# Merge projection of a hybrid decoder layer: from a direct product to Strassen's seven products, with the feed-forward start reordered

## The chip, the cores and the metric

One core of a Trainium2 chip runs the whole kernel. Time is device microseconds of that core for one launch. The engines are TensorE (PE, with its weight loads PEld), VectorE (DVE), ScalarE (ACT), GpSimd (POOL) and SyncE (SP, which here only issues DMAs).

## The reference

The kernel computes one layer for a prompt of 1024 tokens and 8 sample tokens that share the weights, and returns states and caches besides. The part that matters here:

```python
merged = g_a * y_a + g_b * y_b + g_c * y_c          # three gated branches
x = x + merged @ w_merge_o                          # 1024 x 1024
xn = rmsnorm(x, norm_ffn_w)
x = x + (silu(xn @ w_gate) * (xn @ w_up)) @ w_down  # 2816 hidden
y = rmsnorm(x, norm_final_w)
```

All of it is in fp32.

## The kernel before

Activations lie feature by token: 8 tiles of 128 features by 1032 tokens (1024 + 8). The tokens are cut in two halves of 516 (HT, HS), and a half for TensorE into pieces of 256 and 260 columns (HALF). An fp32 product is made as three passes in fp32r: each operand is split into a high part (a copy on ScalarE, written as fp32r) and a low part (the rest, a subtraction on VectorE), and high·high, high·low and low·high are summed in PSUM. `weights` (L161 and on, with its split at L167 and L168) loads a block of 128 output features through SP's queue into one of three raw buffers and splits it; `split_act` (L177, L178) does the same to an activation tile.

The program is written with a framework that keeps tiles in pools, derives the waits, and puts the instructions of each engine in an order of its own; every engine then works through its list in that order. A pool's buffer is only given out again when its last reader is done. The pools named below: `raw`, `whi` and `wlo` (3 each, weights), `ah`/`al` (12 each, high and low parts of activations), `ev` (5, temporaries of 1036 columns), `big` (8 tiles of 1032 columns).

The stages around the change, in the order of time:

1. The attention output (loop at L1788): for each of 8 blocks a product po, multiplied by its gate (L1800) and added to the other branches (L1799, L1801). The results are the 8 tiles `merged` (mg).
2. The merge projection: the 8 tiles are split (mgs); then for half 0 and half 1, and in each for m = 0 to 7, the block's weights are loaded and split again, 8 input tiles × 3 passes × 2 pieces give 48 matmuls into pm (L1869), VectorE adds the residual xT, loaded per block (L1883), ScalarE squares the sum (L1885, L1887), VectorE adds up the squares in sq (L1888), and the block is stored (L1889). The last block of half 1 is done piece by piece (L1879).
3. `norm_half`: the sum of squares over the features by a matmul with ones (psf, L1820), then Ln, Exp and Square on ScalarE (L1822 to L1824) and three rows on VectorE, with rf, the reciprocal root, as the result (L1827). `normed` (L1831) multiplies a block by rf and the norm's weight. For half 0 these, and the forms B11 (blocks 0 to 3) and B21 (blocks 4 to 7) for the feed-forward part, are put in a list (`pend`) from which the loop of half 1 takes one at a time (`tick`). Half 1 is normed at its end.
4. The feed-forward part already works by Strassen's method on pairs of blocks: the 8 input tiles by 2 halves are a 2 by 2 matrix B11, B12, B21, B22, two blocks of weights are the other, and seven products of 24 matmuls (`st_prod`, L267) replace eight. The first 8 blocks (g0, u0, to g3, u3) are begun with the two products that need only half 0, those with B11 and B21 (`st_early`, three at a time); meanwhile half 1 is normed and the forms T1, nT2, T3, B22 and T4 are made (L1928 to L1947, with splits at L393 and L395). Then the pairs follow; the first, g0m, uses the weight sums g0S, g0T and the block g0D (L293 to L300, splits at L254 and L255).

Of the kernel before, what the change touches and what calls it, by code (L numbers as in the profile page):

```python
# [43 lines left out]
def tile_kernel(ctx: ExitStack, tc, a, o):  # L44
# [32 lines left out]
    def flat(ps):  # L77
        return ps.rearrange("p n c -> p (n c)")[:, 252 : 252 + TT]
# [110 lines left out]
    def flush():  # L189
        while pend:  # L190
            tick()
# [66 lines left out]
    def st_ps(tag, name):  # L258
        return pst[0].tile([P, 2, 512], F32, tag=tag, name=name)

    def st_prod(forms, ps, w, off, f, start):
        for kt in range(4):
            xh, xl = forms[f][kt]
            ks = slice(off + kt * P, off + (kt + 1) * P)
            for i, (wt, x) in enumerate(((w[0], xh), (w[0], xl), (w[1], xh))):
                for po, xc in halves_of(ps, x):
                    PE.matmul(  # L267
                        po, wt[:, ks], xc, start=(start and kt == 0 and i == 0), stop=(kt == 3 and i == 2),
                        skip_group_check=True,
                    )  # L270

    def st_early(blocks, forms):

# [1509 lines left out]
    def big(name):  # L1783
        return ph2.tile([P, TT], F32, tag="big", bufs=8, name=name)

    merged = []
    out_in(at_d)
    for m in range(KD):  # L1788
# [3 lines left out]
        merged.append(big(f"mg{m}"))  # L1792
        SY.dma_start(merged[m], mg_d[m])
        yg = ev_tile(f"yg{m}")
        SY.dma_start(yg[:, :TT], yg_d[m])
        gt = ev_tile(f"gt3{m}")
        SY.dma_start(gt[:, :TT], gt_d[16 + m])
        ps = gemm(w, acts, f"po3{m}")
        V.tensor_add(merged[m], merged[m], yg[:, :TT])  # L1799
        V.tensor_mul(gt[:, :TT], flat(ps), gt[:, :TT])  # L1800
        V.tensor_add(merged[m], merged[m], gt[:, :TT])  # L1801
    aux_stack = ExitStack()
    auxp = aux_stack.enter_context(tc.tile_pool(name="aux", bufs=3))

    def aux(name):
        return auxp.tile([P, TT], F32, tag="aux", name=name)

    mg = [split_act(merged[m], f"mgs{m}") for m in range(KD)]


    x2 = [None] * KD
    rfs = [None, None]

    def norm_half(half, sq):
        rfs[half] = out = ev_tile(f"rf{half}")
        t, r = sq[:, :HT], sq[:, HT:TT]
        pss = [sm_ps(f"psf{half}{n}")[:, :HC] for n in range(2)]
        cs = [slice(n * HC, (n + 1) * HC) for n in range(2)]
        for ps, c in zip(pss, cs):
            PE.matmul(ps, ones, sq[:, c], start=True, stop=True)  # L1820
        for ps, c in zip(pss, cs):
            S.activation(t[:, c], ps, AF.Ln, bias=root)  # L1822
        S.activation(r, t, AF.Exp, scale=-0.5)
        S.activation(t, r, AF.Square)  # L1824
        for ps, c in zip(pss, cs):
            V.scalar_tensor_tensor(t[:, c], ps, EPS, t[:, c], op0=ALU.add, op1=ALU.mult)
        V.scalar_tensor_tensor(out[:, :HT], t, -3.0, r, op0=ALU.add, op1=ALU.mult)  # L1827
# [5 lines left out]


    forms = {}
    fx = {}

    def form(f, kt, src, behind=None):
        if kt % 2 == 0:
# [8 lines left out]
    def form_second(kt):  # L1848
        form("B21", kt, normed(kt + 4, 0))

    for half in range(2):
        sq = ev_tile(f"sq{half}")
        for m in range(KD):
            xt = aux(f"xT{half}{m}")
            SY.dma_start(xt[:, :HT], xT_d[m][:, HS[half]])
            wh, wl = weights(wblock(a["w_merge_o"][0], m * P), f"wm{half}{m}")
            if half == 0:
                x2[m] = big(f"x2_{m}")
            t = x2[m][:, HS[half]]

            def merge_part(out, ns):
                for k, (ah, al) in enumerate(mg):
                    if k in (0, 3, 6) and ns[0] == 0:
                        tick()
                    ks = slice(k * P, (k + 1) * P)
                    for i, (wt, x) in enumerate(((wh, ah), (wh, al), (wl, ah))):
                        for n, po in zip(ns, out):
                            lo, hi = HALF[n]
                            PE.matmul(  # L1869
                                po, wt[:, ks], x[:, half * HT + lo : half * HT + hi],  # L1870
                                start=(k == 0 and i == 0), stop=(k == KD - 1 and i == 2),
                            )

            if half == 1 and m == KD - 1:

                for n, (lo, hi) in enumerate(HALF):
                    ps = sm_ps(f"pm{half}{m}{n}")[:, : hi - lo]
                    merge_part([ps], (n,))
                    V.tensor_tensor(t[:, lo:hi], ps, xt[:, lo:hi], op=ALU.add)  # L1879
            else:  # L1880
                ps = mm_ps(f"pm{half}{m}")
                merge_part([hv(ps)[:, lo:hi] for lo, hi in HALF], (0, 1))
                V.tensor_tensor(t, hv(ps), xt[:, :HT], op=ALU.add)  # L1883
            if m == 0:
                S.activation(sq[:, :HT], t, AF.Square)  # L1885
            else:
                S.activation(xt[:, :HT], t, AF.Square)  # L1887
                V.tensor_add(sq[:, :HT], sq[:, :HT], xt[:, :HT])  # L1888
            S.dma_start(x2_d[m][:, HS[half]], t)  # L1889
        if half == 0:  # L1890
            pend.extend([None, None] + [lambda sq=sq: norm_half(0, sq)] + [None])
            for kt in range(4):
                pend.extend([lambda kt=kt: form_first(kt), None, lambda kt=kt: form_second(kt), None])
        else:
            flush()
            norm_half(1, sq)
    aux_stack.close()
    mm_stack.close()

    st_stack = ExitStack()
    pst_stack = ExitStack()
    pst[0] = pst_stack.enter_context(tc.tile_pool(name="pst", bufs=1, space=PSUM))
    pfx = st_stack.enter_context(tc.tile_pool(name="fx", bufs=2))
    fx["T4"] = lambda part, nm: pfx.tile([P, 2, HT], F32R, tag=part, name=nm)


    ffn = {"g": a["w_ffn_gate"][0], "u": a["w_ffn_up"][0]}  # L1910
    early = {}
# [1 line left out]
    for i, (nm, j) in enumerate(((n, j) for j in range(4) for n in "gu")):  # L1913
# [16 lines left out]
    ev_sums = lambda n: ev_tile(n, (P, 1024))  # L1930
# [336 lines left out]
```

## Time and profile before

| what | value |
| --- | --- |
| runs shown, median of 3 | 2428.92 us (2426.12 to 2431.34) |
| profiled execution, its own time | 2428.33 us |
| span of its records | 2426.6 us |
| mean granted clock of TensorE | 0.998 |
| merge projection, first to last matmul (L1869) | 1643.48 to 1736.09 us of the span |

The page gives busy time by engine and the costliest groups. A row of the table of windows is: the window, its length, busy time and instruction count of PE, PEld, DVE, ACT and POOL, then the granted clock, the DMA share and GB/s. A row of a timeline is: start, duration, engine, line, operation, output<-input, shape, count, and in brackets the idle time of the engine before it with what ended it. Durations there overlap where an engine starts the next row before the last one has ended; so the spacing of the starts is the cost.

### The profile page before, as it was taken

To read this page: it belongs to the slowest core of one execution; us is meant where nothing else is said; L and a number is where in the kernel's file an instruction comes from. 1 tells how busy PE (TensorE), PEld (TensorE's weight loads), DVE (VectorE), ACT (ScalarE), POOL (GpSimd) and SP (SyncE) were. 2 spreads that over 40 slices of the span, in tenths; PEclk is the share of its full clock that TensorE was granted. 3 is DMA by queue.
4 is the path that set the end of the run, shared out by engine and by line. 5 is a ranking of instruction groups with operands and counts; after the bars stand their busy time and mean duration, and the time that the engine had idled before them with its cause. 6 is when DMAs were issued, how large, how long until landed. Compare 5 with 4: busy or idle time off the path is not lost. (4 is left out here: it accounts for less than half of the span.)

```text
span 2426.6 us, 45180 instructions
## 1 busy us (share of the span) xinstructions
PE 2397.0 (99%) x18716; PEld 2279.9 (94%) x18716; DVE 1613.8 (67%) x2597; ACT 1091.9 (45%) x1740; POOL 106.9 (4%) x163
## 2 busy tenths in 40 slices
PE   8999999999999999999999999999999999999998
PEld 6999999999999999888888887899999999999998
DVE  6844677777777675568687773454777655567965
ACT  6643555455453543656555542223543333343423
POOL 0000000000000000212212000000000000000000
PEclk9999999999999999999999999999999999999999
DMA  6444423444354345768887797864455333354622
GB/s 203 136 150 164 135 84 114 140 140 131 112 158 118 106 126 179 225 223 272 257 283 215 252 337 234 276 213 150 148 178 168 101 104 103 94 178 154 192 88 79
DMA packets 357716, 407.94 MB, mean 168 GB/s; under 512 B 16270, under 2 KB 277502, under 8 KB 357503
## 3 DMA queue, kind: packets, MB, share of 16 engines
q1 hardware_dynamic: 334374, 341.79, 45.2%
q10 hardware_dynamic: 23137, 63.26, 6.8%
q8 instruction: 147, 2.41, 0.4%
q14 instruction: 58, 0.48, 0.1%
HBM read 288.85 MB, written 116.38 MB: 167 GB/s over the span
## 5 line engine op out<-in xcount | busy, mean ns | idle before, releaser
L1007 ACT ACTIVATE r<-r,acum 128x128 f32<-128x128 f32 x256 | 79.3, 391 | 3.5 <-DMA r<-ac_d 2.6
L796 DVE SCALAR_TENSOR_TENSOR ax<-u,prm,ax 128x1024 f32<-128x1024 f32 x44 | 56.4, 1282 | 0.0
L948 ACT ACTIVATE st<-st,es 128x128 f32<-128x128 f32 x128 | 41.3, 392 | 19.1 <-DMA st<-in_state_ssm_dram 14.5
L1040 POOL TENSOR_TENSOR xdd<-xdt,decst 128x512 f32<-128x512 f32 x32 | 34.3, 1072 | 284.2 <-DVE xdt L1036 278.4
L1034 DVE TENSOR_TENSOR r<-r,cbm 128x1024 f32<-128x1024 f32 x32 | 39.2, 1224 | 4.3 <-ACT r L1009 2.4
L950 DVE SCALAR_TENSOR_TENSOR st<-sr,dts,st 128x128 f32<-128x128 f32 x128 | 41.0, 355 | 0.4
L1059 DVE TENSOR_TENSOR y<-po,ea 128x512 f32<-128x512 f32 x28 | 19.3, 690 | 31.3 <-PE po L1055 31.3
L1076 PE MATMUL pss<-xdd,bT 128*128 128x512 f32 x64 | 34.5, 620 | 3.7 <-ACT bT L1033 3.1
L954 DVE SCALAR_TENSOR_TENSOR sr<-st,sr 128x128 f32<-128x128 f32 x128 | 36.1, 292 | 1.1
L1497 DVE TENSOR_TENSOR yr<-po,yr 128x1032 f32<-128x1032 f32 x8 | 9.8, 1230 | 39.5 <-PE po L218 39.5
L1063 PE MATMUL py<-r,xdt 128*64 128x128 f32 x512 | 35.0, 279 | 0.0
L1009 ACT ACTIVATE r<-r 128x1024 f32<-128x1024 f32 x32 | 33.9, 1058 | 0.7
L1089 POOL TENSOR_TENSOR s<-s,cdec 128x512 f32<-128x512 f32 x28 | 33.1, 1181 | 1.8 <-DVE s L1082 1.5
L1883 DVE TENSOR_TENSOR x<-pm,xT 128x516 f32<-128x516 f32 x15 | 10.4, 694 | 32.3 <-PE pm L1869 32.3
L1800 DVE TENSOR_TENSOR gt<-po,gt 128x1032 f32<-128x1032 f32 x8 | 9.9, 1232 | 32.4 <-PE po L218 31.1
L1063 PEld LDWEIGHTS py<-r,xdt 128*64 128x64 f32 x512 | 27.3, 136 | 4.4 <-issue 1.0
L1055 PE MATMUL po<-bc,s 128*128 128x128 f32 x224 | 29.6, 275 | 0.0
L1055 PEld LDWEIGHTS po<-bc,s 128*128 128x128 f32 x224 | 28.0, 191 | 1.0
L1612 ACT ACTIVATE pr<-psa,mx 128x256 f32<-128x256 f32 x32 | 14.9, 470 | 30.1 <-DVE mx L1610 30.1
L799 DVE SCALAR_TENSOR_TENSOR ax<-u,prm,ax 128x1032 f32<-128x1032 f32 x22 | 28.4, 1290 | 0.0
L1600 DVE SCALAR_TENSOR_TENSOR kc<-kc,qb 128x256 f32<-128x256 f32 x64 | 23.9, 423 | 6.3 <-DMA qb<-qs_d 6.3
L793 ACT ACTIVATE ax<-u,prm 128x1024 f32<-128x1024 f32 x22 | 27.4, 1246 | 1.2 <-ACT u L875 0.4
(9245 smaller groups left out, 8948.9 us busy)
## 6 DMA issues: line engine op xcount, KB each, us to landing
r<-ac_d SPq DMA_DIRECT2D x32, 512.0 KB
gt_d<-G ACTq DMA_DIRECT2D x24, 516.0 KB
gt<-gt_d SPq DMA_DIRECT2D x24, 516.0 KB
xs_d<-ax ACTq DMA_DIRECT2D x22, 516.0 KB
zs<-zs_d SPq DMA_DIRECT2D x16, 516.0 KB
yb_d<-x SPq DMA_DIRECT2D x16, 516.0 KB
in<-yb_d SPq DMA_DIRECT2D x16, 516.0 KB
st<-in_state_ssm_dram SPq DMA_DIRECT2D x32, 256.0 KB
```

The costliest lines, as they stand in the source:

```text
L796: V.scalar_tensor_tensor(acc[:, :T], u[:, j : j + T], w[j], acc[:, :T], op0=ALU.mult, op1=ALU.add)
L948: S.activation(st[:, i], st[:, i], AF.Copy, scale=es[:, g * 4 + i, b : b + 1])
L950: V.scalar_tensor_tensor(st[:, i], rb, dts[:, g * 4 + i, b : b + 1], st[:, i], op0=ALU.mult, op1=ALU.add)
L954: V.scalar_tensor_tensor(rb, st[:, i], 1.0, rc, op0=ALU.mult, op1=ALU.mult, accum_out=ys[:, g * 4 + i, b : b + 1],)
L1007: S.activation(r[:, j, :], r[:, j, :], AF.Relu, scale=-1.0, bias=acum[:, c, h : h + 1])
L1009: S.activation(r, r, AF.Exp, scale=-1.0)
L1034: V.tensor_tensor(r, r, bc(cbm.unsqueeze(1), [P, HPG, P]), op=ALU.mult)
L1040: G.tensor_tensor(b3(xdd, HPG), b3(xdt, HPG), bc(decst[:, c, hs].unsqueeze(2), [P, HPG, 64]), op=ALU.mult)
L1055: PE.matmul(po[:, t * P : (t + 1) * P], state["s"][:, t * P : (t + 1) * P], bcg[1][:, cs], start=True, stop=True,)
L1063: PE.matmul(py[hp : hp + 64, (h // 2) * P : (h // 2 + 1) * P], xdt[:, h * 64 : (h + 1) * 64], r[:, (h % 2) * 4 + h // 2, :], start=True, s ...
L1076: PE.matmul(pss, bT, xdd, start=True, stop=True)
L1089: G.tensor_tensor(b3(s_new, HPG), b3(state["s"], HPG), bc(cdec[:, c, hs].unsqueeze(2), [P, HPG, 64]), op=ALU.mult,)
```

## The change

The merge projection now takes two output blocks at a time as Strassen pairs: the tiles 0 to 3 and 4 to 7 of `merged` by the two halves are B11, B12, B21, B22. From them T1 = B12 − B11, nT2 = T1 − B22, T3 = B22 − B12 and T4 = −nT2 − B21 are formed in place on VectorE (`form_t1` to `form_t4`, L1826 to L1841) and split like other forms (L411 on ScalarE, L413 on VectorE). B11 and T1 are made inside the attention output loop, and so are three quarters of nT2 and B21. Each product of a pair has 24 matmuls (`m_prod`, L1938). The pairs m = 0 and m = 2 come one after the other; the pairs 4 and 6 run together, product by product, in another order (B11, B21, nT2, T3, T4, T1, B22), in which half 0 is finished first. VectorE adds each product to the residual tile or subtracts it (`onto`, L1946); the residual is loaded as a whole block into x2 (`residuals`). `done` squares (L1920), sums (L1921) and stores (L1922). The weight sums of a pair are S and T (L330, L331, L317, L318), or U and X for the last two (L2001 and on).

`norm_half(0)` is now issued between the T1 products of the last two pairs, the forms of half 0 after that, and the first three feed-forward blocks (`st_first`) go kt by kt: g0 and u0 in turn within B11, then g1, then B21 likewise. `norm_half(1)` follows them, and `st_early` does the other five. Ln's table is loaded ahead (L1955). The fx pool is opened before the attention output.

The core of the diff:

```diff
+    def st_first(blocks, ws, forms, tags):
...
+        for off, f, half in ((0, "B11", 1), (512, "B21", 0)):
+            for group in (held[:2], held[2:]):
+                for kt in range(4):
+                    for wA, ps, o1, keep in group:
+                        st_prod(forms, ps, wA, off, f, off == 0, (kt,))
...
         V.tensor_add(merged[m], merged[m], yg[:, :TT])
+        if m == KD - 1:
+            begun = st_begin(wm[0], wm[1], "wm0", ev_sums)
+            for kt in range(3):
+                form_t2(kt)
+            for kt in range(3):
+                mform("B21", kt, merged[kt + 4][:, HS[0]])
         V.tensor_mul(gt[:, :TT], flat(ps), gt[:, :TT])
         V.tensor_add(merged[m], merged[m], gt[:, :TT])
...
-    mg = [split_act(merged[m], f"mgs{m}") for m in range(KD)]
+        if m < 4:
+            form_t1(m)
+    form_t2(3)
+    mform("B21", 3, merged[7][:, HS[0]])
...
-    for half in range(2):
-        sq = ev_tile(f"sq{half}")
-        for m in range(KD):
...
-                ps = mm_ps(f"pm{half}{m}")
-                merge_part([hv(ps)[:, lo:hi] for lo, hi in HALF], (0, 1))
-                V.tensor_tensor(t, hv(ps), xt[:, :HT], op=ALU.add)
...
-        if half == 0:
-            pend.extend([None, None] + [lambda sq=sq: norm_half(0, sq)] + [None])
...
-        else:
-            flush()
-            norm_half(1, sq)
+    for m in (0, 2):
...
+        m_prod(pa, wA, 0, "B11", True)
+        onto(m, 0, pa)
+        wT = st_split(st_adds2(raw1, raw2, sa, nm, ev_sums), nm + "T")
...
+        m_prod(pb, wS, 0, "T1", True)
+        onto(m + 1, 1, pb)
...
+        m_prod(pa, wS, 512, "nT2", False)
+        onto(m, 1, pa)
...
+        m_prod(pc, wA, 512, "B21", True)
+        onto(m, 0, pc)
+        done(m, 0)
+        wD = st_split(raw2[:, 512:], nm + "D", 512)
+        m_prod(pa, wT, 0, "T3", False)
+        onto(m + 1, 1, pa, sub)
+        done(m + 1, 1)
+        m_prod(pb, wT, 512, "B22", False)
+        onto(m, 1, pb, sub)
+        done(m, 1)
+        m_prod(pa, wD, 0, "T4", False)
+        onto(m + 1, 0, pa, sub)
+        done(m + 1, 0)
...
+    for m in last:
+        wX[m] = st_split(sx[m], f"wm{m}X")
+        pbs[m] = whole(st_ps("m0" if m == 4 else "m2", f"wm{m}b"))
+        m_prod(pbs[m], wX[m], 0, "T1", True)
+        if m == 4:
+            norm_half(0)
+        onto(m + 1, 1, pbs[m])
+    firsts = [st_block(wblock(a["w_ffn_gate"][0], 0), "g0")]
+    for kt in range(4):
+        form_first(kt)
+    for m in last:
+        done(m + 1, 1)
+        m_prod(pbs[m], wX[m], 512, "B22", False)
+        onto(m, 1, pbs[m], sub)
+        done(m, 1)
...
-    st_early(blocks, forms)
+    st_first(blocks[:3], firsts, forms, ("m1", "m0", "m2"))
+    norm_half(1)
+    sq_stack.close()
+    st_early(blocks[3:], forms)
```

Three places in VectorE's list. The first is the end of the merge's first block in before: gt37 is the gate of the last attention block, po37 its product, mgs7l the low part of the last merged tile, x2_0 the first result and wm03l the low part of a weight block. In before:

```order
L1800 TENSOR_TENSOR gt37_17711<-po37_17713,gt37_17711 128x1032
L168 TENSOR_TENSOR wm02l_17953<-wm02r_17950,wm02h_17952 128x1024
L1801 TENSOR_TENSOR mg7_17707<-mg7_17707,gt37_17711 128x1032
L178 TENSOR_TENSOR mgs7l_17821<-mg7_17707,mgs7h_17820 128x1032
L1883 TENSOR_TENSOR x2_0_17833<-pm00_17834,xT00_17825 128x516
L168 TENSOR_TENSOR wm03l_18015<-wm03r_18012,wm03h_18014 128x1024
```

In the changed kernel, from the addition of the third product onto x2_0 to the weights of the first pair's T4 (mT40l and mT42l are low parts of T4, mg the merged tiles, wm0a and wm0c PSUM tiles of the first pair):

```order
L1946 TENSOR_TENSOR x2_0_17869<-x2_0_17869,wm0a_17873 128x516
L413 TENSOR_TENSOR mT40l_17989<-mg0_17095,mT40h_17988 128x516
L1841 SCALAR_TENSOR_TENSOR mg1_17193<-mg1_17193,mg5_17564 128x516
L1841 SCALAR_TENSOR_TENSOR mg2_17286<-mg2_17286,mg6_17652 128x516
L1841 SCALAR_TENSOR_TENSOR mg3_17383<-mg3_17383,mg7_17738 128x516
L413 TENSOR_TENSOR mT40l_17989<-mg1_17193,mT40h_17988 128x516
L413 TENSOR_TENSOR mT42l_17997<-mg2_17286,mT42h_17996 128x516
L413 TENSOR_TENSOR mT42l_17997<-mg3_17383,mT42h_17996 128x516
L1946 TENSOR_TENSOR x2_0_17869<-x2_0_17869,wm0c0_17875 128x256
L1946 TENSOR_TENSOR x2_0_17869<-x2_0_17869,wm0c1_17876 128x260
L255 TENSOR_TENSOR wm0Dl_18032<-wm0r2_17820,wm0Dh_18031 128x512
```

The gate's row is the 15th ahead of the first of these. The two forms of rows that the splits of merged had, of 1032 columns, have become rows of 516, and the differences and the additions from PSUM stand among them.

The second place is the norm that the feed-forward start follows. In before this is half 1's, with x2_7's last two pieces, the weights of g1, and psf10, psf11 and rf1 of the norm:

```order
L1879 TENSOR_TENSOR x2_7_18266<-pm170_18799,xT17_18791 128x256
L1879 TENSOR_TENSOR x2_7_18266<-pm171_18825,xT17_18791 128x260
L255 TENSOR_TENSOR g1El_18943<-g1Er_18940,g1Eh_18942 128x1024
L1888 TENSOR_TENSOR sq1_18320<-sq1_18320,xT17_18791 128x516
L1826 SCALAR_TENSOR_TENSOR sq1_18320<-psf10_18855,sq1_18320 128x258
L1826 SCALAR_TENSOR_TENSOR sq1_18320<-psf11_18856,sq1_18320 128x258
L1827 SCALAR_TENSOR_TENSOR rf1_18854<-sq1_18320 128x516
```

In the changed kernel it is half 0's (psf00, psf01, rf0), and behind it come the normed blocks 0 to 3 and the low parts of B11; wm6b and wm4b are PSUM tiles of the last two pairs, which end on blocks 4 to 7:

```order
L1884 SCALAR_TENSOR_TENSOR sq_17866<-psf01_18708,sq_17866 128x260
L1946 TENSOR_TENSOR x2_7_18436<-x2_7_18436,wm6b_18723 128x516
L1885 SCALAR_TENSOR_TENSOR rf0_18706<-sq_17866,rf0_18706 128x516
L1889 SCALAR_TENSOR_TENSOR x2_0_17869<-x2_0_17869,prm_83,rf0_18706 128x516
L1889 SCALAR_TENSOR_TENSOR x2_1_17871<-x2_1_17871,prm_83,rf0_18706 128x516
L1889 SCALAR_TENSOR_TENSOR x2_2_18135<-x2_2_18135,prm_83,rf0_18706 128x516
L1889 SCALAR_TENSOR_TENSOR x2_3_18137<-x2_3_18137,prm_83,rf0_18706 128x516
L413 TENSOR_TENSOR B110l_18757<-x2_0_17869,B110h_18756 128x516
L413 TENSOR_TENSOR B110l_18757<-x2_1_17871,B110h_18756 128x516
L413 TENSOR_TENSOR B112l_18765<-x2_2_18135,B112h_18764 128x516
L413 TENSOR_TENSOR B112l_18765<-x2_3_18137,B112h_18764 128x516
L1946 TENSOR_TENSOR x2_4_18354<-x2_4_18354,wm4b_18681 128x516
```

The addition onto x2_7 now stands inside the norm's chain, and that onto x2_4 behind B11's splits; u0El, the low part of the second feed-forward block's weights, follows right after these rows.

The third place is the start of the first feed-forward pair, where g0sa and g0sb are sums of weights and g0Sl the low part that the first product needs. In before:

```order
L395 TENSOR_TENSOR B222l_19426<-x2_6_18204,B222h_19425 128x516
L395 TENSOR_TENSOR B222l_19426<-x2_7_18266,B222h_19425 128x516
L293 TENSOR_TENSOR g0sa_19369<-g0r2_19367 128x512
L299 TENSOR_TENSOR g0sb_19412<-g0r1_19365,g0r2_19367 128x512
L294 TENSOR_TENSOR g0sa_19369<-g0sa_19369,g0r1_19365 128x512
L300 SCALAR_TENSOR_TENSOR g0sb_19412<-g0sa_19369,g0r1_19365 128x512
L255 TENSOR_TENSOR g0Sl_19373<-g0sa_19369,g0Sh_19372 128x1024
```

In the changed kernel:

```order
L413 TENSOR_TENSOR T30l_19384<-x2_0_17869,T30h_19383 128x516
L311 TENSOR_TENSOR g0sa_19355<-g0r2_19353 128x512
L413 TENSOR_TENSOR T30l_19384<-x2_1_17871,T30h_19383 128x516
L312 TENSOR_TENSOR g0sa_19355<-g0sa_19355,g0r1_19351 128x512
L413 TENSOR_TENSOR T32l_19392<-x2_2_18135,T32h_19391 128x516
L413 TENSOR_TENSOR T32l_19392<-x2_3_18137,T32h_19391 128x516
L317 TENSOR_TENSOR g0sb_19398<-g0r1_19351,g0r2_19353 128x512
L255 TENSOR_TENSOR g0Sl_19359<-g0sa_19355,g0Sh_19358 128x1024
L318 SCALAR_TENSOR_TENSOR g0sb_19398<-g0sa_19355,g0r1_19351 128x512
L413 TENSOR_TENSOR B220l_19406<-x2_4_18354,B220h_19405 128x516
```

Ahead of g0Sl now stand the splits of T3, which in before were long done, and B22's splits have moved behind it.

More of the change, by code (lines that the diff above doesn't have):

```diff
@@ L259, in st_ps, with st_prod @@
         return pst[0].tile([P, 2, 512], F32, tag=tag, name=name)
-    def st_prod(forms, ps, w, off, f, start):
-        for kt in range(4):
+    def st_prod(forms, ps, w, off, f, start, kts=range(4)):
+        for kt in kts:
             xh, xl = forms[f][kt]
@@ L1835, in tile_kernel @@
     forms = {}
-    fx = {}
     def form(f, kt, src, behind=None):
@@ L1897, in tile_kernel, with done @@
[L1897 to L1907, printed above, removed]
+    sq_stack = ExitStack()
+    sqp = sq_stack.enter_context(tc.tile_pool(name="sqp", bufs=1))
+    sq = ev_tile("sq")[:, :TT]
+    started = set()
+    def done(m, half):
+        t, acc = x2[m][:, HS[half]], sq[:, HS[half]]
+        if half not in started:
+            started.add(half)
+            S.activation(acc, t, AF.Square)
+        else:
+            tmp = sqp.tile([P, HT], F32, tag="sqt", name=f"sqt{m}{half}")
+            S.activation(tmp, t, AF.Square)
+            V.tensor_add(acc, acc, tmp)
+        S.dma_start(x2_d[m][:, HS[half]], t)
```

168 lines of the change are left out of this document (126 added, 42 removed).

## The prediction

> **What bounds the kernel now.** I read the page first, then a table of windows, the groups, and last the timelines of single engines around the merge.
>
> ```profile
> PE 2397.0 (99%) x18716; PEld 2279.9 (94%) x18716; DVE 1613.8 (67%) x2597; ACT 1091.9 (45%) x1740; POOL 106.9 (4%) x163
> L1883 DVE TENSOR_TENSOR x<-pm,xT 128x516 f32<-128x516 f32 x15 | 10.4, 694 | 32.3 <-PE pm L1869 32.3
> 1643.48:1736.09 92.61, 92.58 (x775) 92.22 (x775) 53.05 (x67) 35.40 (x46) 0.00 (x0) 1.00 0.54 172
> 1733.00:1790.00 57.00, 56.91 (x475) 56.56 (x474) 42.51 (x63) 34.40 (x54) 0.00 (x0) 1.00 0.50 162
> 1745.00:1765.00 20.00, 20.00 (x170) 20.00 (x169) 20.00 (x30) 11.52 (x19) 0.00 (x0) 1.00 0.42 134
> ```
>
> TensorE is busy 99% of the span. The windows (columns: length; busy time of PE, PEld, DVE, ACT, POOL; granted clock, DMA share, GB/s) say the same of the merge (1643.48 to 1736.09) and of the start of the feed-forward part: 92.58 of 92.61 us, 56.91 of 57.00. In the merge VectorE works 53 of 92.6 us and waits for TensorE (32.3 us at L1883). So a matmul less is time less, as long as VectorE keeps up; and in one stretch, 1745 to 1765, VectorE is full already.
>
> **What goes.** A block's 48 matmuls (wm16, then wm17):
>
> ```profile
> 1724.66 0.41 PE L1869 MATMUL pm<-mgs0h,wm16h 128*128 128x256 f32 x2
> 1730.38 0.28 PE L1869 MATMUL pm<-mgs0h,wm17h 128*128 128x256 f32 x1
> ```
>
> 5.72 us, so 0.1192 each, and 2.86 for a product of 24. Before: 16 blocks, 768 matmuls. After: 4 pairs of 7 products, 672. That is 96 × 0.1192 = **−11.4 us**, all on TensorE.
>
> **What VectorE gets.** Its rows start closer together than they last:
>
> ```profile
> 1703.43 0.69 DVE L1883 TENSOR_TENSOR x<-pm,xT 128x516 f32<-128x516 f32 x1
> 1704.04 0.69 DVE L395 TENSOR_TENSOR B210l<-x,B210h 128x516 fp32r<-128x516 f32 x1
> 1704.64 0.69 DVE L395 TENSOR_TENSOR B110l<-x,B110h 128x516 fp32r<-128x516 f32 x1
> 1705.25 0.69 DVE L1888 TENSOR_TENSOR sq<-sq,xT 128x516 f32<-128x516 f32 x1
> 1705.85 0.75 DVE L1831 SCALAR_TENSOR_TENSOR x<-x,prm,rf 128x516 f32<-128x516 f32 x1
> 1706.52 1.22 DVE L168 TENSOR_TENSOR wm14l<-wm14r,wm14h 128x1024 fp32r<-128x1024 f32 x1
> 1707.65 0.69 DVE L395 TENSOR_TENSOR B210l<-x,B210h 128x516 fp32r<-128x516 f32 x1
> 1792.51 0.69 DVE L299 TENSOR_TENSOR u0sb<-u0r,u0r 128x512 f32<-128x512 f32 x1
> 1793.11 0.69 DVE L381 TENSOR_TENSOR g0o<-g0o,g0m 128x516 f32<-128x516 f32 x1
> 1793.71 0.69 DVE L294 TENSOR_TENSOR u0sa<-u0sa,u0r 128x512 f32<-128x512 f32 x1
> 1794.44 0.69 DVE L300 SCALAR_TENSOR_TENSOR u0sb<-u0sa,u0r 128x512 f32<-128x512 f32 x1
> ```
>
> Start to start: 0.605 for 516 columns, from SBUF or PSUM; 0.60 for 512; 0.67 for a normed row; 1.14 for 1024 (and 1032). L300 needs L294's result and starts 0.73 behind it, 0.125 more: the upper bound of any row. The added rows are of these kinds. Sum over the merge: weight splits 16 × 1.14 become 4 × (3 × 1.14 + 0.60), −2.1; weight sums 16 × 0.60, +9.6; form differences 16 × 0.605, +9.7; form splits 28 × 0.605 for 8 × 1.14, +7.8; additions from PSUM 28 for 16, +7.3. About +32 us, in a merge 11 us shorter. Spread out it would fit beside TensorE (53 + 32 of about 81), but part falls before the merge and the rest comes in three crowds. There I set the rows in program order against TensorE's products.
>
> **First crowd, the first pair.**
>
> ```profile
> 1632.52 1.23 DVE L1800 TENSOR_TENSOR gt<-po,gt 128x1032 f32<-128x1032 f32 x1 [7.81 <-PE po L218]
> 1643.84 1.23 DVE L1800 TENSOR_TENSOR gt<-po,gt 128x1032 f32<-128x1032 f32 x1 [4.38 <-PE po L218]
> ```
>
> Between the last two attention blocks VectorE has 11.32 us. Now 16 rows stand there: 3 × 1.14 + 2 × 0.60 + 11 × 0.605 = 11.3, just full. From the last gt row (0.36 after the merge starts) to mT42l stand 3 × 1.14 + 20 × 0.605 = 15.5; two pieces onto x2_0 (0.7) and wm0Dl (0.6) follow: 17.2. T4 is the seventh product, wanted at 6 × 2.86 = 17.2, its low half a little later. A tie: **+0.2**, from 0 to 0.6.
>
> **Second crowd, the feed-forward start.** In before, half 0 was normed long ahead, and g0 began with its forms ready. Now rf0 comes out of the last pairs. The chain from psf to rf, from before's half 1:
>
> ```profile
> 1739.18 1.14 PE L1820 MATMUL psf<-sq,ones 128*128 128x258 f32 x4
> 1739.96 0.59 PE L267 MATMUL u0e<-B110h,u0Eh 128*128 128x256 f32 x2
> 1739.92 0.91 ACT L1822 ACTIVATE sq<-psf,root 128x258 f32<-128x258 f32 x2 [0.82 <-PE psf L1820]
> 1740.85 1.28 ACT L1823 ACT_TABLE_LOAD   x1
> 1742.14 0.64 ACT L1823 ACTIVATE sq<-sq 128x516 f32<-128x516 f32 x1
> 1742.81 0.64 ACT L1824 ACTIVATE sq<-sq 128x516 f32<-128x516 f32 x1
> 1743.48 0.76 DVE L1826 SCALAR_TENSOR_TENSOR sq<-psf,sq 128x258 f32<-128x258 f32 x2 [4.36 <-ACT sq L1824]
> 1744.27 0.70 DVE L1827 SCALAR_TENSOR_TENSOR rf<-sq 128x516 f32<-128x516 f32 x1
> ```
>
> 5.79 us. Count from the end of wm6's T4 product. TensorE does T1 of wm4 (2.86). Beside it x2_7 (0.9 with its hand-over), a Square (0.64) and the sum (0.7), with g0El (1.14) between, let psf start at about 3.0. To 5.8 come what now stands inside the chain, the Square sqt51 (0.5 on ScalarE) and x2_7 from wm6b (0.6 on VectorE): rf0 at 9.9. Four normed rows (2.7) and B110l (0.6) make 13.3. TensorE has psf (about 1.0) and three products (8.6): it is done at 12.6 and wants B110l 0.24 later: 0.45 lost. Next, u0 takes the PSUM tile that x2_4 still has to be added from; that row stands behind all four B11 splits: 0.4; u0El behind it 0.2; B210h, whose normed row and Square come after, 0.6. g1 loses 0.3. Together **+2.0**.
>
> **Third crowd, the first Strassen pair of the feed-forward.**
>
> ```profile
> 1780.10 1.22 DVE L255 TENSOR_TENSOR g0Sl<-g0sa,g0Sh 128x1024 fp32r<-128x1024 f32 x1 [0.95 <-PE g3e L267]
> 1783.01 0.40 PE L267 MATMUL g0m<-nT20h,g0Sh 128*128 128x256 f32 x2
> 1783.48 0.40 PE L267 MATMUL g0m<-nT20h,g0Sl 128*128 128x256 f32 x2
> 1743.35 0.57 ACT L282 COPY g0e<-g0e 128x516 f32<-128x516 f32 x1
> ```
>
> In before psf of half 1 stood 3.1 us behind the feed-forward start, and g0Sl was ready (1781.3) 2.2 us ahead of its use. Now 80 of the 384 early matmuls stand before psf10. ScalarE's order puts the copy of g1e between Ln and the table load for Exp, and g1e takes 20 more matmuls: psf 1.0, those 2.4, hand-over and copy 0.8, table 1.28, Exp and Square 1.3, the two VectorE rows 1.4: rf1 at psf10 + 8.2, not 5.8. From rf1 to g0Sl stand 44 rows: 6 × 1.14 + 8 × 0.67 + 27 × 0.605 + 3 × 0.60 = 30.3, so g0Sl at psf10 + 38.5. TensorE: 1.0 + 304 × 0.1192 + 0.5 = 37.7. Late by **0.7** with a hand-over. From there to u0Sl 22 rows, 2 × 1.14 + 6 × 0.60 + 14 × 0.605 = 14.3, against five products less the 0.5 done, 13.8: 0.5 more, and 0.2 at u0D. **+1.4**. After that VectorE catches up and the code is the same.
>
> Each wait may also cost TensorE a restart. The trace of before shows no such row for these waits; I bound it by 0 and 0.2 and take 0.1, for a dozen waits **+1.2** (0 to 2.4).
>
> **Sum.** −11.4 + 0.2 + 2.0 + 1.4 + 1.2 = −6.6. The profiled execution took 2428.33, so 2421.7; the shown median, 2428.92, lies 0.6 higher: **2422.3**. Costed at nothing: the residual loads on SP (whole blocks, issued a pair ahead, over 10 us; one that came late would hold only its additions, and TensorE when that PSUM tile is wanted again), eight weight blocks that aren't read twice, the same 16 stores of x2 on ScalarE's queue, ScalarE's added casts (it is busy 35 of 92.6 us in the merge; a late cast would cost what the split behind it costs), and the Ln table loaded early.
>
> "TensorE: Matmul & The Clock Gate" of the Trainium skill (Part 1) says that one idle window of about 3.4 us halves TensorE's clock. By it an 11.4 us gain would be lost if one wait grew that long; by my rows none passes 0.7, and the sum stays.
>
> **Rivals.**
> *No waits at all.* If crowds are absorbed by small slips, the whole 11.4 stays: 2428.92 − 11.4 = 2417.5. For it: the first crowd is a tie. Against: g0Sl has less cover in every count. 0.10.
>
> *Loads come late.* wm4's second weight block and wm6's two must wait for one of three raw buffers, and their rows stand in VectorE's queue ahead of wm2's low halves.
>
> ```profile
> 1602.10 0.32 SPq L1795 DMA_DIRECT2D yg<-yg_d  x1
> 1605.71 1.23 DVE L1799 TENSOR_TENSOR mg<-mg,yg 128x1032 f32<-128x1032 f32 x1 [1.28 <-DMA yg<-yg_d]
> 1785.49 0.82 SPq L1960 DMA_DIRECT2D u0o<-e_d  x1
> 1790.80 0.63 ACT L370 COPY u0o<-u0o 128x516 f32<-128x516 f32 x1 [3.23 <-DMA u0o<-e_d]
> ```
>
> A block of this size landed in 3.6 and in 5.3 us. At 3.6 the three come in time; at 5.3 each holds VectorE up to 1.7 longer, 5.1 in all, of which VectorE's slack takes part: a gain of 1.5 to 4.8, 2424 to 2427.5. The merge moved 172 GB/s at a DMA share of 0.54, which speaks against. 0.23.
>
> *VectorE doesn't overlap its rows (slower).* If a crowd's rows, each reading what a row just ahead wrote, start 0.125 later as L300 does, the first crowd's 42 rows cost 5.2, the second's 24 cost 3.0, the third's 44 cost 5.5: +13.7, time 2436. It decides from 0.06 a row (6.6 / 110) on. Against: only pairs next to each other show it, and the order mostly puts another row between; the 20 us of 1745 to 1765 ran full at 0.605. 0.08.
> "VectorE: DVE Perf Modes" of the Trainium skill (Terms, DRAIN) says that the next operation can't issue until the pipe of the last one is empty. By it every row would cost its whole 0.69, near this rival's time; rows 0.69 long that start 0.605 apart disagree.
>
> *The products aren't fewer.* Excluded: TensorE's list has 17611 rows before, 17515 after.
>
> **Chances.** Forecast (2419 to 2424) 0.55; no waits 0.10; late loads or a larger sum of waits 0.25; slower 0.10 with what I have not seen. 0.2% is 4.9 us, about what a measurement can tell from no change. Faster by more (below 2424.1): 0.65; within: 0.25; slower (over 2433.8): 0.10. The range takes the no-wait case and the late loads with the upper restarts: 2417 to 2429.5.
>
> **What would show it.** Right: 672 products of 2.86 per 24; VectorE full from 11 us before the merge to 17 after; TensorE idle under 1 us at the first T4, 1 to 2 at g0e and u0e, about 1 at g0m and u0m; rf1 some 8 us behind psf10. Wrong: waits of TensorE inside the second and third pairs (late loads), a VectorE row rate above 0.61 (the slower rival), or a granted clock under 1.00 in the merge.

## The result and the profile after

The changed kernel took 2422.85 us (median of 10 runs, 2420.95 to 2427.10), the kernel before 2429.15 (median of 10, 2425.82 to 2434.33). The ratio is 0.9976, 95% interval 0.9966 to 0.9986: about 5.8 us faster, between 3.4 and 8.3. The forecast was 2422.3.

The page of the changed kernel, its first row, and then the table of windows for the merge, for the feed-forward start up to g0m, and for 20 us in which half 1's forms are made (length; busy time of PE, PEld, DVE, ACT, POOL; granted clock, DMA share, GB/s):

```profile
PE 2389.5 (99%) x18620; PEld 2270.1 (94%) x18620; DVE 1644.8 (68%) x2666; ACT 1098.4 (45%) x1761; POOL 105.2 (4%) x163
```

```profile
1645.10:1726.40 81.30, 81.30 (x679) 80.90 (x678) 63.80 (x98) 34.78 (x50) 0.00 (x0) 1.00 0.43 137
1726.40:1775.20 48.80, 47.98 (x391) 46.73 (x390) 43.66 (x66) 33.35 (x52) 0.00 (x0) 1.00 0.44 141
1746.00:1766.00 20.00, 20.00 (x166) 19.61 (x165) 20.00 (x29) 12.04 (x19) 0.00 (x0) 1.00 0.64 205
```

TensorE lost 7.5 us of busy time (9.2 in the next execution of the same code, where the matmuls alone are 11.4) and VectorE gained 31. The merge is 81.2 us long instead of 92.4, with TensorE busy through all of it. VectorE now works 64 of those 81 us, where it worked 53 of 92. The feed-forward start has 0.8 us without a matmul, which it hadn't before. The granted clock stays at 1.00.

All kernels of this study can be read by the lengths of four stages, each from the first matmul of one to the first of the next in the timeline. In the two executions of the changed kernel they differ by less than 0.1 us. The merge of before is counted from its first matmul at 1643.64 us; the 1643.48 of the table ahead of the prediction lies in the stage before it. "To d00m" is the rest of the feed-forward part up to the down projection.

| kernel | merge | g0e to g0m | g0m to u0m | u0m to d00m | sum | median of runs |
| --- | --- | --- | --- | --- | --- | --- |
| before | 92.44 | 46.93 | 14.35 | 393.37 | 547.09 | 2429.15 |
| changed | 81.24 | 48.79 | 15.39 | 394.69 | 540.11 | 2422.85 |
| changed, once more (after_again) | 81.27 | 48.78 | 15.45 | 394.71 | 540.21 | 2422.82 |

The merge gives 11.2 us, and the three stages behind it take back 1.9, 1.0 and 1.3: 7.0 us remain. The spans of the two profiles, 2426.6 and 2423.7 us, differ by some 3 us only, because this execution of the changed kernel reached the merge 1.5 us later and took 2.5 us more from d00m to the end. Most of the latter is one row of PE's waits, which is 1.6 us here and 0.6 in the next execution of the same code (the first run below):

```profile
PE d06m L267 <- DVE x L399: 1.6, 1, 1.6
```

```profile
PE d06m L267 <- DVE x L399: 0.6, 1, 0.6
```

So its length varies from one execution to the next. It is there in every kernel with the new feed-forward start, though: by the spacing of TensorE's starts, 0.5 to 2.2 us are lost at this place in those 13 profiles and 0.3 in the one profile of before. From d00m to the end they take 236.5 to 239.1 us, before 235.9. Some of the 7.0 us may thus be given back in the down projection, which would fit the 6.3 us between the medians. With one profile of before this isn't shown, and its cause stays open.

### The profile page after: what moved, and what is told of

It reads as the page before. It is cut to its first block, busy times and chain, and to the rows that moved or that the text cites. A ratio compares the mean times of both kernels' runs of the same rounds, so it can differ in the third digit from the quotient of the medians.

```text
span 2423.7 us, 45029 instructions
## 1 busy us (share of the span) xinstructions
PE 2389.5 (99%) x18620; PEld 2270.1 (94%) x18620; DVE 1644.8 (68%) x2666; ACT 1098.4 (45%) x1761; POOL 105.2 (4%) x163
## 4 chain that ended last, share of the span: by engine, by line
PE 86%; DMA 5%; DVE 5%; ACT 2%; issue 1%; SPq 0%; DVEq 0%; ACTq 0%
PE po L218 11%; PE ps_q L218 3%; PE py L1081 1%; PE pss L1094 1%; PE ps_z L218 1%; PE po L1073 1%; PE X17m L267 1%; PE G16m L267 1%; PE d00m L267 1%; PE Z2m L267 1%; PE X18m L267 1%; PE Z14m L267 1%; PE Z12m L267 1%; PE Z10m L267 1%; PE Z8m L267 1%
## 5 line engine op out<-in xcount | busy, mean ns | idle before, releaser
L1054 DVE TENSOR_TENSOR xdt<-xp,dtT 128x512 f32<-128x512 f32 x32 | 21.9, 683 | 8.6 <-PE xp L1047 8.5
L1051 ACT COPY bT<-bp 128x128 f32<-128x128 f32 x32 | 8.4, 262 | 39.5 <-DVE cbm L1049 39.4
```

## Where TensorE waits now

Three timelines of the changed kernel, in the order of the forecast's crowds. First the end of the first pair, VectorE's rows and then TensorE's:

```profile
1661.55 0.68 DVE L255 TENSOR_TENSOR wm0Dl<-wm0r,wm0Dh 128x512 fp32r<-128x512 f32 x1
1662.15 0.68 DVE L1946 TENSOR_TENSOR x<-x,wm0a 128x516 f32<-128x516 f32 x1
```

```profile
1662.59 0.40 PE L1938 MATMUL wm2c<-mB210l,wm2Ah 128*128 128x256 f32 x2
1662.88 0.51 PE L1938 MATMUL wm0a<-mT40h,wm0Dh 128*128 128x256 f32 x2
1663.23 0.40 PE L1938 MATMUL wm0a<-mT40l,wm0Dh 128*128 128x256 f32 x2
```

Two matmuls take 0.24, so 0.05 and 0.11 are lost: 0.16 us, the tie. T4's product starts when the addition of T3's product onto x2_1 ends (1662.83): that row frees the PSUM tile wm0a, and it stands behind wm0Dl. T4's own forms were ready by then.

Second, the start of the feed-forward part:

```profile
1722.88 0.69 DVE L1885 SCALAR_TENSOR_TENSOR rf<-sq,rf 128x516 f32<-128x516 f32 x1
1726.28 1.29 DVE L413 TENSOR_TENSOR B110l<-x,B110h 128x516 fp32r<-128x516 f32 x2
```

```profile
1713.88 0.40 PE L1938 MATMUL wm4b<-mT10h,wm4Xh 128*128 128x256 f32 x2
...
1726.38 0.40 PE L267 MATMUL g0e<-B110h,g0Eh 128*128 128x256 f32 x2
1727.02 0.50 PE L267 MATMUL g0e<-B110l,g0Eh 128*128 128x256 f32 x2 [0.24 <-DVE B110l L413]
1727.36 0.40 PE L267 MATMUL g0e<-B110h,g0El 128*128 128x256 f32 x2
1729.02 0.28 PE L267 MATMUL g0e<-B112h,g0Eh 128*128 128x256 f32 x1
1729.43 0.51 PE L267 MATMUL u0e<-B110h,u0Eh 128*128 128x256 f32 x2
1734.50 0.38 PE L267 MATMUL u0e<-B210h,u0Eh 128*128 128x256 f32 x1 [0.44 <-ACT u0e L286]
```

T4's last product ends at 1713.88; rf0 is there 9.7 us later and the first B110l 13.1 us later. The spacing of the starts shows the loss better than the bracket: 1726.38 to 1727.02 is 0.64 for two matmuls, 0.40 lost, and the next step has another 0.10 (0.34 for 0.24). That 0.1 stands behind nearly every wait of this trace: it is the restart.

Third, the first Strassen pair, g0, and the beginning of u0:

```profile
1745.16 0.69 DVE L1885 SCALAR_TENSOR_TENSOR rf<-sq,rf 128x516 f32<-128x516 f32 x1
1774.96 1.22 DVE L255 TENSOR_TENSOR g0Sl<-g0sa,g0Sh 128x1024 fp32r<-128x1024 f32 x1
1790.41 0.70 DVE L406 TENSOR_TENSOR g0o<-g0m,g0o 128x516 f32<-128x516 f32 x1 [1.33 <-PE g0m L267]
1791.03 1.21 DVE L255 TENSOR_TENSOR u0Sl<-u0sa,u0Sh 128x1024 fp32r<-128x1024 f32 x1
```

```profile
1737.69 1.03 PE L1878 MATMUL psf<-sq,ones 128*128 128x256 f32 x4
1775.41 0.40 PE L267 MATMUL g0m<-nT20l,g0Sh 128*128 128x256 f32 x2
1776.23 0.39 PE L267 MATMUL g0m<-nT20h,g0Sl 128*128 128x256 f32 x1 [0.43 <-DVE g0Sl L255]
1791.40 0.40 PE L267 MATMUL u0m<-nT20l,u0Sh 128*128 128x256 f32 x2
1792.29 0.39 PE L267 MATMUL u0m<-T10h,u0Sl 128*128 128x256 f32 x1 [0.50 <-DVE u0Sl L255]
```

rf1 is done 8.2 us after psf10 starts, g0Sl 38.5 us after it, and 0.58 us are lost at g0m. At u0m it is 0.65, after 0.35 for u0Sh (with the restart behind each, 1.2). ScalarE ended u0Sh's cast at 1790.5, but in VectorE's list the row that adds g0m's last product (L406) stands ahead of u0Sl, and it sat 1.33 us waiting for TensorE.

## The experiments

All were timed against the kernel before. The theory: the time of these stages is the number of matmuls plus about 4 us of waits, which VectorE causes in three crowds. The rivals: VectorE sets the pace throughout the merge; or the crowds cost nothing, and what is missing from 11.4 us is chance.

**after_again**: no edit.

> The changed kernel once more, without an edit, as the level for the three runs beside it. If the 2.4 us that its profile showed behind the changed stages (a wait of 1.6 us at d06m in the down projection) belong to the change, they stand here again, at the same place; if they belong to that one execution, the down projection runs as before, and from the first merge matmul to the first one of d00m it takes some 7 us less than before (547.2 us before, 540.2 after).

2422.82 us, ratio 0.9972 (0.9961 to 0.9984). The stages repeat, and the 1.6 us at d06m became 0.6: the wait stands at the same place, and its length belongs to the execution. With the old merge (only_ffn) the same row had 0.4 us.

**extra**: as many matmuls as before.

```diff
-        m_prod(pa, wA, 0, "B11", True)
+        for _ in range(2):
+            m_prod(pa, wA, 0, "B11", True)
```

(and the same in the last two pairs)

> Each pair's B11 product is made twice (the second start overwrites the first): 96 matmuls more, so as many as before the change, and nothing else. Theory (the time of these stages is TensorE's matmuls plus about 4 us of waits): 96 x 0.1192 = 11.4 us more than the changed kernel, less 0 to 0.3 us where VectorE catches up in the first pair: 10.8 to 11.5 more, some 4 to 6 us slower than before the change. Rival (VectorE sets the pace of the merge): the added products fall into waits, and under 8 us are added.

2433.14 us, ratio to before 1.0013 (1.0004 to 1.0021); 10.3 us over the changed kernel by the medians, 10.8 by the stages (92.4, 48.8, 15.4, 394.3): by the stages the lower end of the theory's range, by the medians half a microsecond under it. The merge is then as long as before, 92.4 us in both, although VectorE is busy a fifth longer in it (64.3 us, 53.1 before). So TensorE sets its pace, and what the change costs stands behind the merge.

**rows_full** and **rows_half**: VectorE's price in the first crowd.

```diff
         split_to(*mforms[f][kt], src)
+        if f in ("B22", "T4"):      # rows_half: if f == "T4"
+            hi, lo = mforms[f][kt]
+            V.tensor_sub(lo, src, f32(hi))
```

> Eight VectorE rows more at the first crowd: the low parts of B22 and T4 of the merge are each written twice, the same values. Theory: VectorE is the last there, with no slack (the first pair's T4 product waits for the addition of T3 onto x2_1, which frees its PSUM tile): 8 x 0.605 = 4.8 us more on VectorE give 4.0 to 4.8 us more time, lost by TensorE between the first pair's B22 and T4. Rival (VectorE has slack, the order only looks tight): under 1 us. If each row cost its whole 0.69 us, it would be 5.5 us.

2429.36 us, 6.5 more; the merge took 89.1 us, 7.8 more. More than both theories allow. The timeline of TensorE with one row of VectorE, and two windows behind the first wait (the clock is the third number from the end):

```profile
1659.12 0.40 PE L1941 MATMUL wm0b<-mB222h,wm0Tl 128*128 128x256 f32 x2
1663.26 0.83 PE L1941 MATMUL wm2c<-mB210h,wm2Ah 128*128 128x256 f32 x2 [3.74 <-DVE x L1949]
1663.89 0.63 PE L1941 MATMUL wm2c<-mB210l,wm2Ah 128*128 128x256 f32 x2
...
1688.64 0.69 DVE L2004 TENSOR_TENSOR wm6sx<-wm6r 128x512 f32<-128x512 f32 x1 [2.73 <-DMA wm6r<-in_w_merge_o_dram]
1692.93 0.50 PE L1941 MATMUL wm4c<-mB210h,wm4Ah 128*128 128x256 f32 x2 [0.89 <-DVE x L1949]
```

```profile
1663.50:1669.00 5.50, 5.31 (x24) 5.01 (x25) 5.31 (x8) 2.54 (x4) 0.00 (x0) 0.52 0.93 284
1670.00:1673.00 3.00, 3.00 (x28) 3.00 (x27) 3.00 (x5) 0.81 (x2) 0.00 (x0) 1.00 0.61 222
```

VectorE's rows are still 0.605 apart; the wait is 3.9 us by the spacing, and then TensorE ran 24 matmuls in 5.5 us, where it needs 2.9 at full clock: 2.6 more. Another 1.1 us (by the spacing) is lost at wm4c, because VectorE had waited 2.7 us for wm6's weight block, which the changed kernel waits 0.3 us for: here the prediction's late load cost something. Half the rows tell whether the row price or the clock is behind the 7.8.

> Four VectorE rows more at the first crowd instead of eight: only T4's low parts are written twice. Eight rows cost 7.8 us in the merge stage of the profile (89.1 for 81.3 us), where 8 x 0.605 is 4.8. Theory A (the row price is 0.605, and what is over comes from TensorE's clock: behind the wait of 3.9 us the granted clock was 0.52 for 5.5 us): 4 rows make one or two waits of together 2.4 us, none near 3.9 us, so the clock stays at 1.00 and the merge takes 2.2 to 2.6 us more, 83.5 to 83.9. Theory B (each row costs about 0.98 there, by whatever contention): 3.9 us more, 85.2.

2425.04 us, ratio 0.9987 (0.9976 to 0.9998); the merge took 83.7 us, 2.4 more, which is 4 × 0.605 (by the spacing 1.5 and 0.9 us in its two waits). Theory A. The two waits as the profile's brackets have them, and the clock behind them:

```profile
PE wm2c L1941 <- DVE x L1949: 1.3, 1, 1.3
PE wm0a L1941 <- DVE x L1949: 0.7, 1, 0.7
```

```profile
1664.00:1668.00 4.00, 3.81 (x32) 3.81 (x33) 4.00 (x7) 1.45 (x3) 0.00 (x0) 1.00 0.92 264
```

So a row more in this crowd costs its 0.605 us from the first one on. In rows_full the 3.9 us of the long wait, the 2.6 us of the slow clock and the 1.1 us of the late load make up nearly all of the 7.8.

**rows_slack**: as many rows where VectorE waits.

```diff
+    for m in last:
+        hi, lo = wD[m]
+        for _ in range(4):
+            V.tensor_sub(lo[:, :512], raws[m][1][:, hi_], f32(hi)[:, :512])
     for m in last:
         m_prod(pas[m], wU[m], 0, "nT2", False)
```

> Eight VectorE rows more where VectorE waits for TensorE (the low halves of wm4D and wm6D are each written five times, the same values), 8 x 0.60 = 4.8 us of VectorE between 1697 and 1709 us of the changed kernel's profile, where it stood idle for 6.8 us. Theory: nothing is added (within 0.5 us), because TensorE is last there. Rival (the merge is bound by VectorE's sum, wherever the rows stand): 4 us or more.

2423.05 us, ratio 0.9971 (0.9962 to 0.9981); the stages are those of the changed kernel (81.2, 48.8, 15.4, 394.6). VectorE's sum isn't the limit; its place is.

**seq**: the last two pairs like the first two.

```diff
-    for m in (0, 2):
+    for m in (0, 2, 4, 6):
...
-    last = (4, 6)
...
-        if m == 4:
-            norm_half(0)
...
+    norm_half(0)
     firsts = [st_block(wblock(a["w_ffn_gate"][0], 0), "g0")]
```

> Strassen's products as in the change, but the last two pairs done like the first two, one after the other, and both norms after them: half 0 isn't finished first. Theory: from the last T4 product to B110l TensorE then has nothing: addition, Square and sum about 2.9 us, the chain from psf to rf 5.8, normed rows and the first split 2 to 3: 10 to 12 us idle, of which the second and third crowds' 3.9 us of waits partly go, since psf10 follows at once: 7 to 10 us more than the changed kernel, slower than before. Rival: the order of the last pairs hides little, under 3 us.

2432.76 us, ratio 1.0007 (0.9998 to 1.0016), 9.9 over the changed kernel: not distinguishable from before. The merge with the gap behind it took 91.1 us, 9.8 more, and the stages after it 2.0 less; 1.0 us of this is half 1's psf, which only changes its stage. The three waits of TensorE:

```profile
PE psf L1878 <- DVE sq L1884: 3.6, 1, 3.6
PE psf L1878 <- DVE sq L1921: 2.8, 1, 2.8
PE g0e L267 <- ACT B110h L411: 1.1, 1, 1.1
```

TensorE's clock fell with them: 0.50 in the 4 us behind the longest. Without the order that ends half 0 early, the whole gain of Strassen's products is gone at the norm.

**only_ffn**: the old merge with the new feed-forward start.

```diff
             flush()
-            norm_half(1, sq)
...
-    st_early(blocks, forms)
+    firsts = [st_block(wblock(ffn["g"], 0), "g0"), st_block(wblock(ffn["u"], 0), "u0")]
+    st_first(blocks[:3], firsts, forms, ("m1", "m0", "m2"))
+    norm_half(1, sq)
+    st_early(blocks[3:], forms)
```

> The kernel before with only the feed-forward start changed (g0, u0, g1 kt by kt, norm_half(1) after them), the merge as it was. Theory: that part alone gains nothing, since the forms of half 0 are ready there; rf1 comes some 18 us later, VectorE's list is shorter ahead of g0Sl (32 rows, 21.5 us), so g0Sl is just in time: within 1 us of before. Rival: the late norm makes a crowd of its own, 1.5 us or more slower than before.

2433.99 us, ratio 1.0021 (1.0010 to 1.0032): 5.2 us slower than before, and the theory's figure was wrong. g0Sl was in time (46.6 us to g0m), but the first pair took 20.0 us instead of 14.3. I had counted VectorE's rows up to g0Sl only; T3's and B22's low parts and g0Tl had moved behind it, and so had ScalarE's copy (L353) that frees g0m's PSUM tile. The wait, and the clock behind it:

```profile
PE g0m L267 <- ACT g0o L353: 2.7, 1, 2.7
```

```profile
1789.50:1794.00 4.50, 4.48 (x24) 4.48 (x25) 4.50 (x8) 3.52 (x7) 0.00 (x0) 0.62 0.38 121
```

By the spacing the wait is 2.9 us; another 1.0 is lost at g0's T4 product, where the trace names no cause, and most of the rest of the 5.6 is the clock. The late norm is a cost by itself. The changed kernel pays less of it, as far as its place explains: psf10 stands there ahead of g1e's matmuls, behind 80 early matmuls; here behind 144.

**blocks**: the first feed-forward blocks one after the other.

```diff
-            for group in (held[:2], held[2:]):
+            for group in (held[:1], held[1:2], held[2:]):
```

> The first three feed-forward blocks one after the other in each form, instead of g0 and u0 in turn, kt by kt; PSUM tiles and the rest as they are. Theory: TensorE waits there (1.9 us in all at the feed-forward start) for u0's PSUM tile, u0El and B21's splits, which block after block are wanted 2 to 3 us later, while g0 needs a new low part only every 0.72 us and VectorE makes one every 0.605; so the start's loss falls from 1.9 to about 1.0, and the time by 0.5 to 1.0 us. Rival (kt by kt is what hides the late forms): g0 then waits for B11's splits itself, and the time rises by 1 us or more.

2423.06 us, ratio 0.9980 (0.9971 to 0.9989); 49.2 us from g0e to g0m instead of 48.8. Neither theory: the wait for u0's PSUM tile went, but u0El's grew to 0.5 us, B21's stayed (0.6), and a new one of 0.8 us came at g2El. psf10 stands at the same place (80 early matmuls before it, 11.3 us behind the first of g0e), but in ScalarE's list u1Eh's cast and two copies now stand ahead of the norm's Square, and in VectorE's u1El ahead of its rows: rf1 comes 1.8 us later, and g2El stands behind it. The turn-taking is worth 0.4 us in this stage and 0.3 in the next.

**norm_early**: half 1's norm issued earlier.

```diff
-    st_first(blocks[:3], firsts, forms, ("m1", "m0", "m2"))
-    norm_half(1)
+    st_first(blocks[:3], firsts, forms, ("m1", "m0", "m2"), lambda: norm_half(1))
```

(`st_first` calls it after its first group)

> norm_half(1) is issued after the first two feed-forward blocks' B11 products instead of after all three blocks; in the lists psf10 comes 14 matmuls earlier and the table load for Exp ahead of g1e's copy. Theory: g0Sl's lateness comes from rf1; rf1 2 to 4 us earlier gives g0Sl its cover back, the waits at g0m (0.6 us) and u0m (0.9 us) go or halve: 0.7 to 1.5 us less time. Rival: VectorE is full from rf1 on whatever the start, because rows that now stand ahead of it move behind it; then g0Sl comes at the same time and nothing changes (within 0.3 us).

2421.50 us, ratio 0.9979 (0.9970 to 0.9988), not to be told from the changed kernel's 0.9972; the stages add up to 539.7, 0.4 less. Counted from g0e's first matmul, rf1 came 3.3 us earlier and g0Sl 0.6:

```profile
1738.08 0.70 DVE L1888 SCALAR_TENSOR_TENSOR rf<-sq,rf 128x516 f32<-128x516 f32 x1
1770.55 1.22 DVE L255 TENSOR_TENSOR g0Sl<-g0sa,g0Sh 128x1024 fp32r<-128x1024 f32 x1
```

VectorE was busy 34.6 of the 35 us between: g0sb's two rows and two of B22's splits now stood ahead of g0Sl. The rival is the nearer one: the waits at g0m (0.5 us) and u0m (0.7) stayed, and the 0.4 comes from u1e's wait, which is gone.

**pool**, **pool_sq**, **pool_sq_norm**: rows given to GpSimd. The first moves the sums g0sa, g0sb and u0sa, u0sb (all but the last row of sb):

```diff
-        V.tensor_add(sa[:, 512:], sa[:, :512], raw1[:, :512])
+        (G if nm in ("g0", "u0") else V).tensor_add(sa[:, 512:], sa[:, :512], raw1[:, :512])
```

the second also moves sums of squares, the third adds the edit of norm_early:

```diff
-            V.tensor_add(acc, acc, tmp)
+            (G if half == 1 and m >= 4 else V).tensor_add(acc, acc, tmp)
```

> Three of the four weight sums of g0 and of u0 made on GpSimd, which idles there, instead of VectorE; in VectorE's list u0Sl then stands ahead of the row that waits for g0m's T4 product (L406), behind which it stood in the changed kernel. Theory: the waits at g0m (0.7 us with restart) and u0m (1.2 us) are VectorE's, the second by that place in its list: g0Sl comes 1.2 to 1.8 us earlier and u0Sl over 2, both waits go, first feed-forward pair 14.4 instead of 15.4 us: 1.2 to 1.9 us less time than the changed kernel. Rival (VectorE stays full and other rows fill the gap, as with the earlier norm): under 0.5 us.

> As the run pool, and the last four additions of squares of half 1 on GpSimd too. Theory: these four rows stand among the normed blocks and B21's splits at the feed-forward start, so without them B21's wait (0.7 us) falls to nothing: 48.8 becomes 47.5 to 48.2 us from g0e to g0m, another 0.5 to 1.0 us. Rival: GpSimd's rows last about 1.1 us instead of 0.6 and form one chain, so psf10 and rf1 come later and the first pair waits again: no gain over pool, or a loss of up to 1 us.

> As pool_sq, and norm_half(1) issued as early as in norm_early. Theory: with VectorE relieved the earlier rf1 is used: nothing waits at g0m and u0m, first pair 14.4 us, 1.9 to 2.8 us less time in all than the changed kernel, about 2420. Rival: psf10 now stands in TensorE's list before the additions on GpSimd are done, and TensorE waits for it, 0.5 to 1.5 us, which takes the gain away.

2428.34, 2431.75 and 2429.68 us, ratios 1.0002 (0.9993 to 1.0011), 1.0012 (1.0003 to 1.0021) and 1.0005 (0.9996 to 1.0013): all three gave the gain back. No theory held. Of the rivals only the last came near: TensorE does wait at psf10, but 3.4 us by the spacing, not 0.5 to 1.5. In pool, GpSimd's three rows for g0, and VectorE's rows around the first one's end, with one more from the time of u0's sums:

```profile
1763.82 6.90 POOL L311 TENSOR_TENSOR g0sa<-g0r 128x512 f32<-128x512 f32 x1 [456.10 <-ACT g3e L300]
1770.68 1.28 POOL L317 TENSOR_TENSOR g0sb<-g0r,g0r 128x512 f32<-128x512 f32 x1
1771.91 1.26 POOL L312 TENSOR_TENSOR g0sa<-g0sa,g0r 128x512 f32<-128x512 f32 x1
```

```profile
1768.27 1.29 DVE L413 TENSOR_TENSOR T32l<-x,T32h 128x516 fp32r<-128x516 f32 x2
1773.21 0.69 DVE L318 SCALAR_TENSOR_TENSOR g0sb<-g0sa,g0r 128x512 f32<-128x512 f32 x1 [3.64 <-POOL g0sa L312]
...
1778.38 1.78 DVE L413 TENSOR_TENSOR B222l<-x,B222h 128x516 fp32r<-128x516 f32 x1
```

The first sum lasted 6.90 us while VectorE ran ten rows without a pause (until 1769.6), and the next 1.3 once VectorE stood still. The delay also goes the other way: the row of B222l lasted 1.78 us instead of 0.69 while GpSimd made u0sa, which took 1.73. "SBUF — State Buffer" of the Trainium skill (section "SBUF: two separate sides") says that VectorE with two SBUF inputs and a GpSimd operation that reads SBUF take a shared port by an exclusive lock, whichever starts first, and the other one is blocked. This trace agrees that they block each other; that VectorE keeps GpSimd out over ten of its rows is what the 6.90 us show. The u0m wait did go (u0m to d00m 393.6 instead of 394.7), as the place of u0Sl in the list promised, but g0m waited 3.8 us, and the clock fell again (0.64 over the next 4 us). In the other two, TensorE also waited at psf10 for the additions on GpSimd.

No version of these beats the changed kernel beyond the measurement.

## Why the prediction was right

**The matmuls.** 96 × 0.1192 = 11.4; the profiles count 18716 and 18620 instructions on TensorE, 96 apart, and the merge stage became 11.2 us shorter, 0.16 of the difference being the tie at T4. extra shows it from the other side.

**VectorE's row prices and the counting of rows.** rf1 to g0Sl: 30.3 us counted, 30.3 measured (1745.85 to 1776.2). rf0: 9.9 counted, 9.7 measured; B110l: 13.3 (its terms add up to 13.2) and 13.1; rf1: 8.2 behind psf10, and 8.2; g0Sl: 38.5 and 38.5. The 0.605 spacing held in every crowd, so the slower rival (0.125 more a row) is out.

**First crowd, +0.2.** 0.16, and rows_half and rows_full show that there is no slack behind it. The waiting dependency was another than I named: the PSUM tile, not T4's low half.

**Second crowd, +2.0.** The stage became 1.9 us longer. The waits at g0e, u0e and B21's splits are 1.8 with their restarts, and 0.5 stand at u1e, which I had not foreseen; g1e, for which I had 0.3, waited for nothing. The stage before had a little of its own (0.25 ahead of psf). With a restart for each of its waits the forecast had some 2.5 here, 0.6 too much.

**Third crowd, +1.4.** The wait at g0Sl was 0.7 with its restart, as counted. u0's were 1.2 instead of 0.5, and here the mechanism I gave was incomplete: I compared sums of rows (14.3 against 13.8) and overlooked that the row of L406 waits for TensorE's last product ahead of u0Sl. u0D's was 0.1. Another 0.3 stands at u2m's T4 product (0.24 and its restart of 0.11), for which I had nothing: VectorE's addition of u2m's T3 product ends only at 1860.95 us, behind the weight rows of g3, just ahead of that product's start. So the two stages became 2.4 us longer, where the forecast with its restarts had some 1.7.

**Restarts, +1.2.** 0.1 each, as taken, and some ten of them, 1.0; they are in the numbers above. The 0.1 was a choice between two bounds, and that it is exact is luck.

Together the waits were to cost 4.8 us and cost 4.5 (0.24 in the merge, then 1.86, 1.05 and 1.32 by the stages; of the last, 0.9 are u0m's waits, 0.1 u0D's and 0.3 u2m's). The sum, −6.6, came out as −7.0 by the stages and −6.3 by the medians. That it is so close is in part luck: the second crowd was forecast too high by about as much as the third was too low, and the interval of the measurement, 3.4 to 8.3 us, would not have told a miss of 2 us. The prediction put nothing on the time behind u0 ("the code is the same"); u2m's 0.3 us and the wait at d06m stand there.

**The rivals.** No waits at all would have given 2417.5: out. Late loads: VectorE waited 1.2 us for wm4's second block and 0.3 for wm6's, and TensorE for neither, so the cover held; in rows_full, where VectorE waited 2.7 us for wm6's, it didn't quite. That one long wait would halve the clock didn't happen in these stages, since none of the change's waits passed 0.8 with its restart, and the 1.6 us at d06m left the clock at 1.00; it did happen in rows_full, only_ffn, seq and pool. The prediction's sentence that the whole 11.4 us would then be lost was too strong: in rows_full the long wait and the slow stretch behind it cost 6.5 us together.

## What to carry to other kernels

When the bounding engine is relieved by giving another one more to do, set that engine's rows, in program order, against the times at which the bounding engine wants them; the sum over the stage hides where it is late, and the count must run on past the first consumer, to the next pair and to the rows that free PSUM tiles. A norm between two matmul stages can decide whether fewer matmuls are worth anything: here, without half 0 finished early, the gain was gone. Moving rows to an idle engine only helps if it can run beside the full one; here it couldn't.

## What the runs showed of the hardware

A wait of TensorE of 2.7 us (only_ffn) and of 3.7 us (rows_full) was followed by 4.5 and 5.5 us at about half the granted clock (0.62 and 0.52 in the windows above), in which TensorE did 1.6 and 2.6 us less than at full clock. Waits up to 1.7 us left it at 1.00 (1.3 and 0.7 in rows_half, 1.6 at d06m). Around 2 us both happened: 2.0 us at d06m in pool_sq brought the clock to 0.65 over the next 4 us, while waits of 2.1 us in an earlier stage of seq and of rows_slack left it at 1.00. "TensorE: Matmul & The Clock Gate" of the Trainium skill (Part 1) gives an idle window of about 3.4 us for this; here 2.0 and 2.7 us were enough.

A GpSimd row with SBUF inputs made almost no headway beside a VectorE that ran two-input rows without a pause: 6.90 us against 1.3 (pool), and 5.79 against 1.3 in pool_sq. Elsewhere the two slowed each other: 1.73 us for a row of GpSimd, 1.78 for one of VectorE that alone takes 0.69.
